# A first gather with the one-hot rows held still, products of no use in the routing's waits, and p loaded in another step

## The chip, the cores and the metric

The kernel runs on one core of one Trainium2 chip. Its time is what the device takes for one launch, in microseconds; of several runs the median is given. TensorE (PE in the rows, with its weight loads as PEld), VectorE (DVE), ScalarE (ACT), GpSimd (POOL) and SyncE (SP) run their own instructions in their own order and wait for each other by semaphores. SP issues nearly all transfers, on one queue.

## The reference, cut to what matters

One layer over 512 tokens of 1024 channels, in float32:

```
merged = sigmoid(gate_pool) * (A @ w_pu) + sigmoid(gate_attn) * (B @ w_au)
x   = LayerNorm(alpha * x + merged @ w_o)
moe = for each token: top 1 of 4 groups, then top 2 of its 8 experts;
      h = silu(x @ w_eg[e]) * (x @ w_eu[e]);  y += (h @ w_ed[e]) * weight
ple = sigmoid(x @ w_pg) * (p @ w_pp)
x   = LayerNorm(alpha * x + moe + ple)
```

There are 32 experts, each with 6 MB of weights (`w_eg` and `w_eu` are 1024 x 512, `w_ed` is 512 x 1024). All of them are read whatever the tokens choose. p has 512 x 256 numbers, `w_pg` 1024 x 1024.

## The kernel before, in words

Tokens stand in four blocks of 128. Most operands outside the experts are kept as two parts, high and low (type fp32r in the rows), whose products are added. Up to 343 us the kernel makes the projections, both mixers and the output projection, whose last blocks are interleaved with the first norm and the routing.

**Routing** (lines 910 to 1001, in an order written out by hand). `normalise` scales a block; `turn` transposes it; `route` multiplies it by the router's weights; `keep_high` (ACT) and `keep_low` (an engine named by the caller) store its high and low parts in `x1`, in the order that the experts' weights want. `choose` finds group and experts for two blocks at a time on DVE and ends with `msk`, the 0/1 choice; `place` counts a token's place in its expert by products with a triangle of ones; `one_hots` makes `G`, 0/1 rows that say which token goes to which slot. `count_tokens` and `rank` order the experts by tokens, `weigh` makes the weights, `relabel` turns both into the order by rank.

**Gather.** A unit has 128 slots, for two, three or four experts. `gather` multiplies: x1's 128 channels are the stationary operand and `G`, 128 slots wide, is moved, so the result has channels in partitions, as the experts' products need it. For unit 0 that is 8 channel blocks x 4 token blocks x 2 parts = 64 products. Four PSUM banks are opened by a product with zeros each (`open_bank`), half of the sum is made before blocks 2 and 3 are chosen (around `choose` and `place`), the rest behind `one_hots` of these blocks. `keep_slots` scales and shifts the result into `xg`. The first expert product (`inner(0, 0)`) follows in pieces.

**Experts** (`pair`). There are twelve units: `inner` makes h's two factors with the slots stationary and the weights moving, 8 k-steps each; four transposes turn h; `outer` makes the output, whose pieces are added to `acc` by `scatter_steps` in the next unit. In even units the next two units' slots are gathered between the outer products: two banks behind f = 1, two behind f = 3. In units 0 and 1 `renew` builds `acc` anew from `x1`.

**Weights.** Each expert comes in six chunks of 1 MB. A chunk's load is issued by SP when `eload_past` is told that TensorE has used up an older chunk, into that one's buffer. Loads stand on SP in the order in which the code calls for them. Sixteen buffers serve, of which eight are of the kind `s8`; the dictionary `KEEP` says from which step (unit, place in the unit) on how many of these eight are withheld from the chunks.

**Embedding** (`embedding`, a generator). `EMB` says how many of its steps run at each of six places of a unit: 0 between the halves of the first product, 1 behind it, 2 between the halves of the second, 3 behind h's transposes, 4 behind f = 1, 5 at the end. Step 1 loads p (`pr`) and begins to add x1's parts on POOL; step 2 transposes p and loads the first quarter of `w_pg` and `w_pp`; steps 3 to 6 transpose x1; step 7 makes high and low parts of the quarter (`split`: a copy on ACT, a subtraction on POOL) and loads the next one; then four steps of products, and so on for four quarters.

Of the kernel before, what the change touches and what calls it, by code (L numbers as in the profile page):

```python
# [37 lines left out]
def layer_kernel(ctx: ExitStack, tc: tile.TileContext, x, p, w_in, w_pool, pool_scale, w_pu, w_au,  # L38
# [18 lines left out]
    def mm(name="mm"):  # L57
        return ps.tile([128, 512], F32, name=name, tag="mm", bufs=4)
# [625 lines left out]

    def rank(ct, at, rcol):

        o = zz("rk_ps")
        nc.tensor.matmul(o[:, :E], ecol[:E].to_broadcast([E, 128]), at[:E], start=True, stop=True)
        nc.tensor.matmul(o[:, E:2 * E], rcol[:E].to_broadcast([E, 128]), ident[:E, :E], start=True, stop=True)
        nc.vector.tensor_copy(order, o[:, :E])  # L690
        rk, over = (lnt.tile([128, E], F32, name=n, tag=t) for n, t in (("rk", "fold"), ("over", "i8")))
        nc.vector.tensor_copy(rk, o[:, E:2 * E])

        nc.vector.tensor_scalar(room, rk, BIG - 0.5, float(CAP // 2), op0=OP.is_lt, op1=OP.mult)
        nc.vector.tensor_scalar(over, rk, E - FIXED - 0.5, float(CAP // 2), op0=OP.is_gt, op1=OP.mult)
        nc.vector.scalar_tensor_tensor(room, room, float(CAP // 2), over, op0=OP.add, op1=OP.add)
        nc.vector.tensor_sub(over, ct[:, :E], room)
        countf = lnt.tile([128, 1], F32, name="countf")
        nc.vector.tensor_reduce(countf, over, axis=AX.X, op=OP.max)
        nc.vector.tensor_scalar(countf, countf, 0.0, None, op0=OP.max)  # L700
        nc.vector.tensor_copy(count, countf)
        return rk

# [128 lines left out]

    def gather(G, o, kb, tbs):

        whole = len(tbs) == NT
        n = G[0].shape[2] * 128
        for kx in range(2):
            cs = slice((2 * kb + kx) * 128, (2 * kb + kx + 1) * 128)
            for tb in tbs:
                for i in range(2):  # L840
                    nc.tensor.matmul(o[:, kx * 256:kx * 256 + n], x1[tb][:, i, cs],  # L841
                                     G[tb // 2][:, tb % 2].rearrange("p u s -> p (u s)"),
                                     start=whole and tb == i == 0,
                                     stop=tb == NT - 1 and i == 1 and (whole or kx == 1))

    def open_bank(o):

        nc.tensor.matmul(o, strict[:, :1].to_broadcast([128, 128]), strict[:, None].to_broadcast([128, 4, 128]),
                         start=True, stop=False)

# [59 lines left out]
    with tc.manual_schedule():  # L910
# [47 lines left out]
        normalise(3)  # L958
        xs = [mm("xg_ps") for _ in range(4)]
        for o in xs:  # L960
            open_bank(o)
        route(2)
        keep_high(1, (1,))
        keep_low(1, 0, pool)
        keep_low(1, 1, dve)
        one_hots(G[0], (0,), 0)
        turn(3)
        keep_high(2)
        keep_low(2, 0, pool)
        route(3)  # L970
        xtp_cm.__exit__(None, None, None)
# [4 lines left out]
        fold_logits(lg2, 3)  # L976
        for kb in range(2):
            gather(G, xs[kb], kb, (0, 1))
        keep_high(3)
        keep_low(2, 1, dve)  # L980
        choose(lg2, 2)
        keep_low(3, 0, pool)
        place(2)
        keep_low(3, 1, dve)
        eload_first(17)
        for kb in range(2, 4):
            gather(G, xs[kb], kb, (0, 1))
        G.append(lnt.tile([128, 2, 1, 128], F32R, name="G", tag="wr2"))
        one_hots(G[1], (0,), 2)
        counted = count_tokens()  # L990
        slots_of((0,))
        for kb in range(4):
            gather(G, xs[kb], kb, (2, 3))
            keep_slots((0,), xs[kb], kb)
            if kb == 1:
                first = mm()
                rk = rank(*counted)
            if kb:
                inner(0, 0, first, range(2 * kb - 2, 2 * kb))
        inner(0, 0, first, range(6, 8))  # L1000
        relabel(rk, weigh())
# [6 lines left out]
    def pair(j, other, extra):  # L1008
# [76 lines left out]
        for f in range(4):  # L1085
            for c in range(2):
                outer(j, hT, f, c, o[c])
            if f % 2:
                eload_past(chunk0[j] + n_experts[j] * (4 + (f + 1) // 2))
            if m and f % 2:  # L1090
                og = [zz("xg_ps") for _ in range(2)]
                for i in range(2):
                    gather(G, og[i], f - 1 + i, range(NT))
                    keep_slots(m, og[i], f - 1 + i)
            if f == 1:
                embed(4)
                Gt, ws = turn_one_hots(Gw)
        embed(5)
        y = [weighted(o[c], ws) for c in range(2)]
# [47 lines left out]
    def embedding():  # L1147
# [58 lines left out]
        def split(raw):  # L1206
            hi = s8([128, KD, 256], F32R, "pgh"), ex.tile([128, 2, 256], F32R, name="pph", bufs=1)
            lo = s8([128, KD, 256], F32R, "pgl"), ex.tile([128, 2, 256], F32R, name="ppl", bufs=1)
            for r, h, l in zip(raw, hi, lo):
                nc.scalar.activation(h, r, AF.Copy)  # L1210
                nc.gpsimd.tensor_sub(l, r, h.bitcast(F32))  # L1211
            return hi, lo
# [56 lines left out]

    EMB = {3: (0, 0, 0, 1, 0, 0), 4: (1, 1, 1, 1, 1, 1), 5: (2, 2, 1, 2, 2, 1), 6: (2, 2, 1, 2, 1, 1)}  # L1270

    KEEP = {(2, 5): 2, (3, 1): 4, (3, 5): 5, (4, 0): 6, (4, 1): 7, (4, 2): 8}
    with tc.manual_schedule():
# [124 lines left out]
```

## Time and profile before

| | us |
|---|---|
| median of three runs | 877.06 (876.9 to 878.21) |
| profiled execution, its own time | 878.82 |
| its span in the trace | 877.1 |
| mean granted TensorE clock | 0.956 |

PE is busy 812.8 us of the span, DVE 429.1, ACT 228.4, POOL 174.5. The queue of SP carries 241.11 MB. A granted clock of 1.00 is 2.4 GHz, 0.50 is 1.2 GHz. In the rows a matmul in plain float32 (the experts' products) stands as two records; those of the high and low parts as one. A matmul's time in a row runs to the end of its pipeline, so neighbours overlap, and a group of them takes less than the sum. A number in brackets at the end of a row is the engine's idle time before it, and behind the arrow who ended it. The chain that ended last shows for a transfer when it was issued and how long it took to land, its time in the queue with it.

### The profile page before, as it was taken

To read this page: it belongs to the slowest core of one execution; us is meant where nothing else is said; L and a number is where in the kernel's file an instruction comes from. 1 tells how busy PE (TensorE), PEld (TensorE's weight loads), DVE (VectorE), ACT (ScalarE), POOL (GpSimd) and SP (SyncE) were. 2 spreads that over 40 slices of the span, in tenths; PEclk is the share of its full clock that TensorE was granted. 3 is DMA by queue.
4 is the path that set the end of the run, shared out by engine and by line. 5 is a ranking of instruction groups with operands and counts; after the bars stand their busy time and mean duration, and the time that the engine had idled before them with its cause. 6 is when DMAs were issued, how large, how long until landed. Compare 5 with 4: busy or idle time off the path is not lost.

```text
span 877.1 us, 11632 instructions
## 1 busy us (share of the span) xinstructions
PE 812.8 (93%) x4454; PEld 515.6 (59%) x4454; DVE 429.1 (49%) x746; ACT 228.4 (26%) x471; POOL 174.5 (20%) x165
## 2 busy tenths in 40 slices
PE   8999899899999999998999778799899999999983
PEld 7886677677768887734354334476375744545422
DVE  5278647545458756457742446322113243443337
ACT  3123444444461115213202011220211201210314
POOL 3333324224221222100002020212313000000135
PEclk9999999999999999599999988899899999999997
DMA  7431131212114695576999999999999999999992
GB/s 252 142 97 49 48 96 49 82 63 87 58 49 167 178 382 206 228 287 247 421 420 419 417 406 419 371 405 375 418 411 399 407 419 418 420 420 419 412 370 99
DMA packets 66076, 241.91 MB, mean 276 GB/s; under 512 B 12384, under 2 KB 32864, under 8 KB 41696
## 3 DMA queue, kind: packets, MB, share of 16 engines
q1 hardware_dynamic: 66016, 241.11, 70.7%
q8 instruction: 37, 0.61, 0.3%
q14 instruction: 23, 0.19, 0.1%
HBM read 239.00 MB, written 2.10 MB: 275 GB/s over the span
## 4 chain that ended last, share of the span: by engine, by line
PE 29%; DMA 18%; DVE 2%; issue 2%; POOL 1%; ACT 1%; SPq 1%; POOLq 0%; DVEq 0%; ACTq 0%
PE mm L905 11%; DMA ew<-in_w_eu_dram 8%; PE mm L1110 7%; DMA ew<-in_w_eg_dram 4%; PE xg_ps L841 4%; DMA ew<-in_w_ed_dram 3%; PE sc_ps L1143 3%; DMA pr<-in_p_dram 2%; PE pg_ps L143 1%; PE pg_ps L144 1%; PE pg_ps L145 1%; POOL pgl L1211 1%; SPq L538 0%; PE hT_ps L1057 0%; PE gt_ps L882 0%
## 5 line engine op out<-in xcount | busy, mean ns | idle before, releaser
L905 PE MATMUL mm<-ew,xg 128*32 128x512 f32 (+1 forms) x1088 | 189.6, 632 | 12.2 <-DMA ew<-in_w_eu_dram 8.6
L905 PEld LDWEIGHTS mm<-ew,xg 128*32 128x32 f32 (+1 forms) x1088 | 54.5, 126 | 132.4 <-issue 107.7
L1110 PE MATMUL mm<-ew,hT 128*32 128x512 f32 (+1 forms) x544 | 93.2, 611 | 2.1 <-DMA ew<-in_w_ed_dram 1.1
L143 PE MATMUL mm<-xth,whi 128*128 128x512 f32 x224 | 91.6, 409 | 0.0
L132 POOL TENSOR_TENSOR wlo<-wraw,whi 128x1024 fp32r<-128x1024 f32 x23 | 69.0, 3000 | 106.3 <-DVE whi L127 52.2
L145 PE MATMUL mm<-xth,wlo 128*128 128x512 f32 x224 | 88.7, 396 | 0.0
L144 PE MATMUL mm<-xtl,whi 128*128 128x512 f32 x224 | 88.3, 394 | 0.0
L1042 DVE TENSOR_TENSOR h<-mm,h 128x512 f32<-128x512 f32 x24 | 16.6, 692 | 106.8 <-PE mm L905 55.5
L841 PEld LDWEIGHTS xg_ps<-G,x 128*128 128x128 f32 x448 | 59.6, 207 | 15.5 <-issue 12.3
L841 PE MATMUL xg_ps<-G,x 128*128 128x256 f32 (+1 forms) x448 | 62.6, 300 | 2.4 <-DVE xg L861 2.4
L1144 DVE TENSOR_TENSOR acc<-acc,sc_ps 128x512 f32<-128x512 f32 x88 | 54.7, 682 | 6.6 <-PE sc_ps L1143 6.0
L1110 PEld LDWEIGHTS mm<-ew,hT 128*32 128x32 f32 (+1 forms) x544 | 25.1, 122 | 54.7 <-issue 47.5
L143 PEld LDWEIGHTS mm<-xth,whi 128*128 128x128 f32 x224 | 42.8, 191 | 9.5 <-issue 0.9
L144 PEld LDWEIGHTS mm<-xtl,whi 128*128 128x128 f32 x224 | 43.0, 192 | 8.8 <-issue 0.5
L145 PEld LDWEIGHTS mm<-xth,wlo 128*128 128x128 f32 x224 | 42.6, 190 | 9.4
L859 ACT ACTIVATE xg<-xg_ps,bq,gq 128x128 f32<-128x128 f32 x56 | 24.7, 456 | 89.2 <-PE xg_ps L841 79.5
L127 DVE CAST whi<-wraw 128x2048 fp32r<-128x2048 f32 x22 | 26.9, 1225 | 33.8 <-PE mm L144 16.6
L132 DVE TENSOR_TENSOR wlo<-wraw,whi 128x1024 fp32r<-128x1024 f32 x23 | 40.7, 1769 | 1.0
L144 PE MATMUL pg_ps<-pgl,xT 128*128 128x256 f32 x128 | 37.0, 289 | 4.0 <-POOL pgl L1211 4.0
L1159 POOL TENSOR_TENSOR xf<-x 128x1024 f32<-128x1024 f32 x4 | 9.4, 2371 | 149.4 <-PE mm L905 120.9
L1231 DVE TENSOR_TENSOR sg<-pg_ps,sg 128x256 f32<-128x256 f32 x16 | 6.8, 425 | 66.0 <-ACT sg L1230 66.0
L1143 PE MATMUL sc_ps<-yh,Gt 128*128 128x512 f32 x88 | 37.8, 430 | 1.1 <-DVE sg L1231 1.1
(269 smaller groups left out, 1357.8 us busy)
## 6 DMA issues: line engine op xcount, KB each, us to landing
ew<-in_w_eg_dram SPq DMA_DIRECT2D x64, 1024.0 KB, 15.3
ew<-in_w_eu_dram SPq DMA_DIRECT2D x64, 1024.0 KB, 14.0
ew<-in_w_ed_dram SPq DMA_DIRECT2D x62, 1024.0 KB, 14.0
wraw<-in_w_in_dram SPq DMA_DIRECT2D x15, 1024.0 KB, 5.6
wraw<-in_w_o_dram SPq DMA_DIRECT2D x4, 1024.0 KB, 5.0
pgr<-in_w_pg_dram SPq DMA_DIRECT2D x4, 1024.0 KB, 16.4
wraw<-in_w_pu_dram SPq DMA_DIRECT2D x2, 1024.0 KB, 4.9
wraw<-in_w_au_dram SPq DMA_DIRECT2D x2, 1024.0 KB, 5.0
```

The costliest lines, as they stand in the source:

```text
L127: nc.vector.tensor_copy(hi, wraw[i])
L132: eng.tensor_sub(lo[:, j], wraw[i][:, j], hi[:, j].bitcast(F32))
L143: nc.tensor.matmul(o, lh, rh, start=start, stop=False)
L144: nc.tensor.matmul(o, lh, rl, start=False, stop=False)
L145: nc.tensor.matmul(o, ll, rh, start=False, stop=stop)
L841: nc.tensor.matmul(o[:, kx * 256:kx * 256 + n], x1[tb][:, i, cs], G[tb // 2][:, tb % 2].rearrange("p u s -> p (u s)"), start=whole and tb ...
L859: nc.scalar.activation(xgs[us[0]][:, k], o[:, i, 0], AF.Identity, scale=gq[:, k:k + 1], bias=bq[:, k:k + 1])
L905: nc.tensor.matmul(o[cs], xgs[j][:, k, cs], ew[chunk0[j] + ne * (2 * n + k // 4) + i][:, k % 4], start=k == 0, stop=k == KD - 1)
L1042: nc.vector.tensor_mul(ht, o, ht)
L1110: nc.tensor.matmul(o[cs], hT[:, f, cs], ew[chunk0[j] + ne * (4 + f // 2) + i][:, f % 2, halves[c]], start=f == 0, stop=f == 3)
L1143: nc.tensor.matmul(o, Gt[:, tb * 128:(tb + 1) * 128], y[c][i], start=i == 0, stop=i == 1)
L1144: nc.vector.tensor_add(acc[tb][:, cs], acc[tb][:, cs], o)
```

## The change

The first gather is turned round: `gather_rows` holds the one-hot rows of a token block still (128 tokens x 128 slots) and moves 512 channels of `x1`, so the result has slots in partitions, in two banks. `turn_rows` then transposes it, in two halves of four transposes, and scales and shifts it into `xg`, alternately on ACT and DVE. The first expert product follows in one piece.

`busy(n)` runs n products of 512 columns into a bank that nobody reads: four before `route(2)`, four before `turn(3)`, five before `route(3)`, ten before `place(2)`, three before the second half of the gather. Two `keep_low` calls move from DVE to POOL, so that POOL has four in a row. `rank` is split: the capacity check (`measure`) runs behind the first expert product in the code.

In unit 0 the gathers for units 1 and 2 come behind all outer products, with one bank at a time. In `split`, half of the `w_pg` subtraction goes to DVE. p's step moves from unit 3, place 3, to unit 3, place 0; the first `split` from unit 4, place 5, to place 4; `KEEP` withholds buffers earlier.

```diff
-    def rank(ct, at, rcol):
+    def rank(at, rcol):
...
+        rk = lnt.tile([128, E], F32, name="rk", tag="fold")
         nc.vector.tensor_copy(rk, o[:, E:2 * E])
+        return rk
+
+    def measure(ct, rk):
...
-    def open_bank(o):
-        nc.tensor.matmul(o, strict[:, :1].to_broadcast([128, 128]), strict[:, None].to_broadcast([128, 4, 128]),
-                         start=True, stop=False)
+    def gather_rows(G, o, c, tbs):
+        for tb in tbs:
+            for i in range(2):
+                nc.tensor.matmul(o[c], G[tb // 2][:, tb % 2, 0], x1[tb][:, i, halves[c]], start=tb == i == 0,
+                                 stop=tb == NT - 1 and i == 1)
+
+    def turn_rows(rows, h):
+        pt = tt("xgT_ps")
+        for k in range(4):
+            nc.tensor.transpose(pt[:, k * 128:(k + 1) * 128], rows[:, (4 * h + k) * 128:(4 * h + k + 1) * 128], ident)
+        for i in range(4):
+            k = 4 * h + i
+            src, g, b = pt[:, i * 128:(i + 1) * 128], gq[:, k:k + 1], bq[:, k:k + 1]
+            if i % 2:
+                nc.vector.tensor_scalar(xgs[0][:, k], src, g, b, op0=OP.mult, op1=OP.add)
+            else:
+                nc.scalar.activation(xgs[0][:, k], src, AF.Identity, scale=g, bias=b)
+
+    def busy(n):
+        for _ in range(n):
+            nc.tensor.matmul(spare, strict, strict[:, None].to_broadcast([128, 4, 128]), start=True, stop=True)
...
-        xs = [mm("xg_ps") for _ in range(4)]
-        for o in xs:
-            open_bank(o)
+        spare = mm("spare_ps")
+        xs = [mm("xg_ps") for _ in range(2)]
+        busy(4)
         route(2)
...
         one_hots(G[0], (0,), 0)
+        busy(4)
         turn(3)
         keep_high(2)
         keep_low(2, 0, pool)
+        busy(5)
         route(3)
...
-        for kb in range(2):
-            gather(G, xs[kb], kb, (0, 1))
         keep_high(3)
-        keep_low(2, 1, dve)
+        keep_low(2, 1, pool)
+        for c in range(2):
+            gather_rows(G, xs, c, (0, 1))
         choose(lg2, 2)
         keep_low(3, 0, pool)
+        keep_low(3, 1, pool)
+        busy(10)
         place(2)
-        keep_low(3, 1, dve)
         eload_first(17)
-        for kb in range(2, 4):
-            gather(G, xs[kb], kb, (0, 1))
...
-        for kb in range(4):
-            gather(G, xs[kb], kb, (2, 3))
-            keep_slots((0,), xs[kb], kb)
-            if kb == 1:
-                first = mm()
-                rk = rank(*counted)
-            if kb:
-                inner(0, 0, first, range(2 * kb - 2, 2 * kb))
-        inner(0, 0, first, range(6, 8))
+        rows = lnt.tile([128, D], F32, name="rows")
+        busy(3)
+        for c in range(2):
+            gather_rows(G, xs, c, (2, 3))
+            if c:
+                nc.vector.tensor_copy(rows[:, halves[c]], xs[c])
+            else:
+                nc.scalar.activation(rows[:, halves[c]], xs[c], AF.Copy)
+        turn_rows(rows, 0)
+        rk = rank(*counted[1:])
+        turn_rows(rows, 1)
+        first = mm()
+        inner(0, 0, first, range(KD))
+        measure(counted[0], rk)
         relabel(rk, weigh())
...
-            if m and f % 2:
+            if m and j and f % 2:
...
+        if j == 0:
+            for kb in range(4):
+                og = zz("xg_ps")
+                gather(G, og, kb)
+                keep_slots(m, og, kb)
         embed(5)
...
-            for r, h, l in zip(raw, hi, lo):
+            parts = [(t[0][:, :4], t[0][:, 4:], t[1]) for t in (raw, hi, lo)]
+            for r, h, l, eng in zip(*parts, (nc.gpsimd, nc.vector, nc.gpsimd)):
                 nc.scalar.activation(h, r, AF.Copy)
-                nc.gpsimd.tensor_sub(l, r, h.bitcast(F32))
+                eng.tensor_sub(l, r, h.bitcast(F32))
...
-    EMB = {3: (0, 0, 0, 1, 0, 0), 4: (1, 1, 1, 1, 1, 1), 5: (2, 2, 1, 2, 2, 1), 6: (2, 2, 1, 2, 1, 1)}
-    KEEP = {(2, 5): 2, (3, 1): 4, (3, 5): 5, (4, 0): 6, (4, 1): 7, (4, 2): 8}
+    EMB = {3: (1, 0, 0, 0, 0, 0), 4: (1, 1, 1, 1, 2, 0), 5: (2, 2, 1, 2, 2, 1), 6: (2, 2, 1, 2, 1, 1)}
+    KEEP = {(2, 2): 2, (3, 1): 4, (3, 3): 5, (3, 5): 6, (4, 0): 7, (4, 1): 8}
```

## Rows read from the trace of the kernel before

**Rows 1.** Stages; busy us of each engine, then granted clock, DMA share, GB/s
```profile
353.00:366.00 13.00, 12.25 (x57) 12.09 (x58) 7.16 (x31) 2.63 (x4) 1.54 (x1) 0.50 0.82 318
366.00:376.60 10.60, 10.60 (x32) 4.61 (x31) 1.59 (x11) 1.61 (x4) 0.00 (x0) 0.50 0.01 5
...
412.00:541.00 129.00, 115.22 (x702) 49.94 (x691) 64.58 (x110) 18.45 (x31) 9.39 (x4) 0.93 1.01 411
541.00:700.00 159.00, 145.46 (x1086) 96.21 (x1082) 42.97 (x85) 29.45 (x51) 34.19 (x23) 0.96 0.99 398
700.00:850.00 150.00, 146.65 (x797) 67.28 (x798) 60.24 (x99) 24.19 (x46) 10.36 (x9) 0.99 1.01 417
```

**Rows 2.** Timeline of SP's issues: start us, us, engine, line
```profile
376.62 1.25 SPq L538 DMA_DIRECT2D ew<-in_w_eg_dram  x2
...
567.23 0.58 SPq L1153 DMA_DIRECT2D pgr<-in_w_pg_dram  x1
```

**Rows 3.** Timeline of PE, routing and unit 0; idle before in brackets
```profile
344.58 1.16 PE L848 MATMUL xg_ps<-strict 128*128 128x512 f32 x4
...
347.55 1.37 PE L594 MATMUL x1T_ps<-ident,acc 128*128 128x128 f32 x8 [0.47 <-ACT acc L769]
...
353.31 3.65 PE L841 MATMUL xg_ps<-G,x 128*128 128x128 f32 x16
...
367.41 3.68 PE L905 MATMUL mm<-ew,xg 128*64 128x512 f32 x8
...
377.57 10.52 PE L905 MATMUL mm<-ew,xg 128*64 128x512 f32 x48
...
404.40 4.07 PE L841 MATMUL xg_ps<-G,x 128*128 128x256 f32 x32 [2.42 <-DVE xg L861]
```

**Rows 4.** Timeline of PE in unit 4
```profile
507.55 1.94 PE L1188 MATMUL pT_ps<-ident,pr 128*128 128x128 f32 x8 [8.73 <-DMA pr<-in_p_dram]
...
528.55 1.94 PE L905 MATMUL mm<-ew,xg 128*32 128x512 f32 x8 [4.38 <-DMA ew<-in_w_eu_dram]
```

**Rows 5.** The page's costliest groups: busy us, mean ns, then idle before
```profile
L1042 DVE TENSOR_TENSOR h<-mm,h 128x512 f32<-128x512 f32 x24 | 16.6, 692 | 106.8 <-PE mm L905 55.5
...
L859 ACT ACTIVATE xg<-xg_ps,bq,gq 128x128 f32<-128x128 f32 x56 | 24.7, 456 | 89.2 <-PE xg_ps L841 79.5
...
L144 PE MATMUL pg_ps<-pgl,xT 128*128 128x256 f32 x128 | 37.0, 289 | 4.0 <-POOL pgl L1211 4.0
```

**Rows 6.** Timeline of DVE, routing of blocks 2 and 3, relabelling
```profile
349.36 1.06 DVE L782 TENSOR_TENSOR x<-acc,x 128x512 fp32r<-128x512 f32 x1 [2.71 <-ACT x L779]
...
352.15 1.74 DVE L782 TENSOR_TENSOR x<-acc,x 128x512 fp32r<-128x512 f32 x1 [0.20 <-ACT x L779]
...
354.61 0.96 DVE L641 CAST gif<-gi 128x2 f32<-128x2 uint32 x1
...
357.35 0.22 DVE L655 TENSOR_TENSOR msk<-oh 128x64 fp32r<-128x64 f32 x1
...
378.73 0.25 DVE L712 RECIPROCAL rc<-sgm 128x16 f32<-128x16 f32 x1 [9.42 <-ACT sgm L711]
...
383.86 0.29 DVE L740 TENSOR_TENSOR ranked<-by_slot 128x128 f32<-128x128 f32 x1
```

**Rows 7.** Timeline of POOL
```profile
351.30 1.55 POOL L782 TENSOR_TENSOR x<-acc,x 128x512 fp32r<-128x512 f32 x1 [3.09 <-ACT x L779]
354.01 1.54 POOL L782 TENSOR_TENSOR x<-acc,x 128x512 fp32r<-128x512 f32 x1 [1.16 <-ACT x L779]
...
562.70 4.51 POOL L1211 TENSOR_TENSOR pgl<-pgr,pgh 128x2048 fp32r<-128x2048 f32 x1 [48.37 <-DMA ew<-in_w_eg_dram]
```

**Rows 8.** Chain that ended last: start us, us, what
```profile
468.62 19.84 DMA ew<-in_w_eg_dram
488.48 18.94 DMA pr<-in_p_dram
...
510.06 18.44 DMA ew<-in_w_eu_dram
```

More of the change, by code (lines that the diff above doesn't have):

```diff
@@ L690, in rank @@
         nc.vector.tensor_copy(order, o[:, :E])
-        rk, over = (lnt.tile([128, E], F32, name=n, tag=t) for n, t in (("rk", "fold"), ("over", "i8")))
+        rk = lnt.tile([128, E], F32, name="rk", tag="fold")
         nc.vector.tensor_copy(rk, o[:, E:2 * E])
+        return rk
+    def measure(ct, rk):
+        over = lnt.tile([128, E], F32, name="over", tag="i8")
         nc.vector.tensor_scalar(room, rk, BIG - 0.5, float(CAP // 2), op0=OP.is_lt, op1=OP.mult)
@@ L701, in rank @@
         nc.vector.tensor_copy(count, countf)
-        return rk
     def weigh():
@@ L831, in one_hots, with gather @@
                                         pos[:, b:b + 2, :, None].to_broadcast(shape), op=OP.is_equal)
-    def gather(G, o, kb, tbs):
-        whole = len(tbs) == NT
+    def gather(G, o, kb):
         n = G[0].shape[2] * 128
@@ L838, in gather @@
             cs = slice((2 * kb + kx) * 128, (2 * kb + kx + 1) * 128)
-            for tb in tbs:
+            for tb in range(NT):
                 for i in range(2):
@@ L842, in gather @@
                                      G[tb // 2][:, tb % 2].rearrange("p u s -> p (u s)"),
-                                     start=whole and tb == i == 0,
-                                     stop=tb == NT - 1 and i == 1 and (whole or kx == 1))
-    def open_bank(o):
-        nc.tensor.matmul(o, strict[:, :1].to_broadcast([128, 128]), strict[:, None].to_broadcast([128, 4, 128]),
-                         start=True, stop=False)
+                                     start=tb == i == 0, stop=tb == NT - 1 and i == 1)
+    def gather_rows(G, o, c, tbs):
[17 more added lines that the diff above has]
+            nc.tensor.matmul(spare, strict, strict[:, None].to_broadcast([128, 4, 128]), start=True, stop=True)
     def slots_of(us):
@@ L1089, in pair @@
                 eload_past(chunk0[j] + n_experts[j] * (4 + (f + 1) // 2))
-            if m and f % 2:
+            if m and j and f % 2:
                 og = [zz("xg_ps") for _ in range(2)]
                 for i in range(2):
-                    gather(G, og[i], f - 1 + i, range(NT))
+                    gather(G, og[i], f - 1 + i)
                     keep_slots(m, og[i], f - 1 + i)
```

## The prediction

> **What bounds the kernel now.** I read the table by stages first. From 412 us to 850 us the DMA share stays near 1.0 at 398 to 417 GB/s [rows 1]: the experts' weights arrive at the rate the queue can give, and the end follows the last of them. So microseconds count where the queue runs dry, and the same table shows where: from 366.0 to 376.6 its share is 0.01 [rows 1]. Every weight buffer is full then, and the next load is issued at 376.62, when unit 0's first four k-steps have ended on TensorE [rows 2]. What holds TensorE back is the second thing to see in the table: its granted clock is 0.50 (the lower level, 1.2 GHz) from 353 to 376.6 [rows 1], while it is busy almost without a break. Before that it had short idle stretches behind the last transposes (one of 0.47 us in [rows 3]) and narrow products. Third come the waits later on: 8.73 us until p has landed, 4.38 us for an expert chunk [rows 4], 4.0 us for POOL's subtraction of the embedding weights [rows 5]. Because the queue is full there, they cost time only as far as they empty it.
>
> The profiled execution took 878.82 us (span 877.1, so 1.7 us lie around it), 1.76 us over the median of 877.06. I work out a difference against the span and take it from the median.
>
> **First gather, up to the first expert product.** It now takes 16 products of 512 columns in place of 64 of 128 columns. Before, 16 narrow ones took 3.65 us at the lower clock [rows 3], so 64 cost 14.6 us, half of them behind the second half of the routing. A wide one at full clock: four took 1.16 us [rows 3], less the tail that overlaps, about 0.25 us each. So 2.1 us for eight, and eight of the sixteen lie beside the choice of experts, as the old ones did.
>
> Now the path, counted from the release of `msk`. The choice of experts ends at 357.35 + 0.22 = 357.57 [rows 6]; the first half of unit 0's first product ends when the load at 376.62 is issued [rows 2]: 19.05 us. Afterwards, at full clock:
> - place, positions, one-hots: 1.5 us. They took 357.57 to about 360.3, with one `keep_low` in between (1.06 us a piece [rows 6]) that moves to POOL, and with their products at half clock.
> - counting and the three products of no use: 0.6 us more on TensorE. (The four at first take the place of four that opened banks, 1.16 us [rows 3]; four and five more fill waits for ACT and DVE.)
> - eight wide products 2.1 us; the second half's copy out of PSUM 0.7 (a 128x512 one takes 692 ns on DVE [rows 5]); four transposes 0.6 (eight took 1.37 with a wait in them [rows 3]).
> - four k-steps, 16 records: 48 took 10.52 us [rows 3], so 3.5 us.
>
> Sum 9.0 us, a saving of 10.0. The other four k-steps took 3.5 us at full clock already, but in the old order 1.0 us of gather stood between (376.6 to 377.57 [rows 2, 3]): the first product is ready 11.0 us sooner. The scaling copies from the transposes are new. ACT and DVE share a bank and will probably alternate, 8 x 0.46 us [rows 5] = 3.7 us, but TensorE needs 0.88 us per k-step (four records), so it stays the slower of the two and hides them. Without that cover they would cost 3.2 us, all but the first.
>
> `choose` starts about 0.4 us sooner, since the 1.74 us subtraction in front of it leaves DVE [rows 6]. The ten products of no use (2.5 us) end at about 357.3 and lie beside `choose`; so they cost nothing at full clock. But four subtractions now run on POOL back to back, and that has a price. The DVE subtraction at 352.15 took 1.74 us against 1.06 at 349.36, and ended 1.06 us after POOL's own one ended at 352.85; the cast at 354.61 took 0.96 us and ended with POOL's at 355.55 [rows 6, 7]. So DVE's two-input operations and casts wait for POOL's. `choose` has seven such, POOL three subtractions left: from nothing to 2 x 1.55 = 3.1 us more. I take 0.2, near the lower end, since POOL's subtractions are few and most of `choose` is one-input work; so 11.0 + 0.4 - 0.2 = 11.2 us, with the ends 8.3 and 12 (the 0.6 us of counting hidden).
>
> The Trainium skill (GPSIMD Engine Reference, section Specifications) says that POOL shares its SBUF interfaces with VectorE, in contention with instructions of two SBUF inputs or in a two-port mode. The trace agrees (1.74 against 1.06 us); by the rule each of the seven could wait, so its sum is 8.3.
>
> **What follows in unit 0.** DVE's rank, capacity and relabelling work goes behind the copies: about 1.3 + 0.5 us, then 378.73 to 384.15, 5.4 us [rows 6]. It ends near 372.5, before unit 0's second product (about 376.7), so it stays hidden; it has 3 us of slack before SiLU is late. Gathering for units 1 and 2 behind all of unit 0's outer products: TensorE waited 2.42 us there for DVE's scaling [rows 3], which is queued behind the renewal of x1. DVE sets this end before and after, so it is worth 0 for TensorE; two chunks are loaded some 4 us sooner, but the queue runs dry behind them again until unit 1's first product. So 11.2 us arrive at 412 unchanged.
>
> **p and the embedding.** p's load moves from j = 3, step 3 to step 0. It was issued at 488.48 and landed 18.94 us later, behind a queue 20 us deep [rows 8]. In unit 3's first half it stands behind the fourth of unit 4's first eight loads; the second was issued at 468.62 [rows 8] and they go out every 2.5 us, so p goes at about 476 (in old time) and lands near 496, ahead of the transposes (507.55 - 8.73 = 498.8 [rows 4]): the 8.73 us wait goes. POOL's additions that move with it find POOL idle. What is late next is the expert chunks: p passes five of them, which land its 1.25 us later, so that those for the next half are there at 468.62 + 19.84 + 6 x 2.5 + 1.25 = 504.7, the next four at 515, and the last of the second product at 510.06 + 18.44 = 528.5, where TensorE waited 4.38 us anyway [rows 4, 8]. The queue was full throughout (1.01 [rows 1]). So this is worth 0; ends -1 (two buffers less from j = 2 on) and +2.
>
> `split` gives half of the 4.51 us subtraction [rows 7] to DVE, and its first one moves ahead of unit 4's last outer products. That takes away the 4.0 us wait [rows 5] and lets SP pass: SP issued the next embedding load at 567.23 only, when POOL was done [rows 2], with loads behind it. In return four expert loads now stand behind that issue and come about 2 us later. In 541 to 700 the queue moved 398 GB/s against 417 later [rows 1]: 159 x (1 - 398/417) = 7.2 us lost in all. I follow it through unit 5: embedding load and four chunks are in at about 574 in both orders, the next group comes 1.9 us sooner, and the one after 2.5. I take 2.3; ends -1 and 6.
>
> **Sum:** 11.2 + 0 + 2.3 = 13.5 us, 877.06 - 13.5 = 863.6. From 700 on TensorE has hardly a wait and the queue is full [rows 1]; both start sooner by the same amount, and the tail is unchanged.
>
> **Rivals.**
> - The clock falls all the same, for a while, between 352 and 360. For it: route's products stay narrow. Against it: 13 wide products fill the stretches, and wide expert products, begun at 367.41, were what TensorE ran when the clock came back [rows 1, 3]. Up to 5 us of work stretches to twice its length: 3 us less, 866.6. Chance 0.14. The Trainium skill (TensorE: Matmul & The Clock Gate, Part 1) lays the clock to how busy the engine is. The trace bears out half: from 353.31 to 367.41 TensorE was busy with narrow products nearly without a break, and the clock stayed at 0.50 [rows 1, 3].
> - POOL holds DVE at every operation: 2.9 us less (3.1 for 0.2), 866.5. Chance 0.12.
> - p and the embedding free the queue fully: 16 to 17 us in all, 860.5. For it: 7.2 us are lost there. Against it: the loads of pg. Chance 0.09.
> - Slower: the clock stays at half through the whole path and the products of no use become its longest part. Eight wide and ten useless ones from 353.3 on take 18 x 0.43 = 7.7 us, so TensorE reaches `place` at 361.0, not 357.3; place, positions and one-hots until 363.0, counting and three more until 365.2, eight wide until 368.9, copy and transposes until 370.5. Eight k-steps at half clock (8 records took 3.68 us [rows 3], 32 take 14.7) end at 385.2 against 381.1 before: +4.1 us, 881.2. It decides from a granted clock of 0.50 that still stands at 378. Against it: wide expert products were running when the clock came back. Chance 0.04.
> - It doesn't do what it says (a buffer conflict stalls the gather, worth about 11 us): 877. Chance 0.03.
>
> **Chances.** The forecast has 0.58, at 861 to 866. Faster by over 0.2% (1.75 us, what can be told from no change) 0.93, within it 0.03, slower 0.04. The range 859 to 869 takes in the rivals but the last two, and most of a clock that falls for longer.
>
> **What would show it.** Right: granted clock 1.00 through 353 to 377; next load issued near 366; dry time before it 1 to 3 us, not 11; the gathers for units 1 and 2 ended near 397 (404.40 + 4.07 = 408.5 before [rows 3]); no wait for p, but waits for chunks near 493 and 504 instead; no 4 us wait for `pgl`. Wrong: a clock of 0.50 after 353, casts of over a microsecond in `choose`, a DMA share under 0.95 between 412 and 530, or the time from 700 to the end changed.

## The result and the profile after

The changed kernel takes 868.02 us (median), the kernel before beside it 877.63. Three executions in this document were disturbed and count in no ratio: one of the four of the changed kernel here (1118 us; the others lie from 867.4 to 868.04), one of the kernel before in the first group of experiments (3615 us), and one of the experiment on unit 0's gather (1300 us). The ratio of the two kernels is 0.9886, with 0.9867 to 0.9905 as the 95% interval. So the change is faster, by 9.6 us between the medians, and the forecast of 863.6 was 4.4 us too low: inside the range of 859 to 869, above the 861 to 866 that had a chance of 0.58. The profiled execution took 868.04 us (span 866.3, 10.8 less than the span before).

The stages of the changed kernel, in the columns of [rows 1]:

```profile
353.00:366.00 13.00, 11.34 (x59) 8.34 (x61) 9.35 (x35) 3.98 (x7) 4.45 (x3) 1.00 0.80 315
366.00:376.60 10.60, 10.60 (x52) 3.56 (x50) 7.31 (x28) 1.16 (x4) 0.00 (x0) 1.00 0.72 273
...
412.00:541.00 129.00, 114.75 (x660) 51.53 (x656) 62.93 (x120) 20.14 (x35) 9.35 (x4) 0.98 1.02 417
541.00:700.00 159.00, 148.49 (x1090) 93.50 (x1084) 49.83 (x79) 28.48 (x52) 30.05 (x24) 0.99 0.99 403
```

The granted clock is 1.00 where it was 0.50, and the stretch in which the queue was dry, 366 to 376.6, now has a DMA share of 0.72 instead of 0.01. SP's issues of the changed kernel show the new place of the first late load and of the embedding's load:

```profile
368.10 3.77 SPq L538 DMA_DIRECT2D ew<-in_w_eg_dram  x3
...
547.89 0.59 SPq L1185 DMA_DIRECT2D pgr<-in_w_pg_dram  x1
549.66 2.58 SPq L538 DMA_DIRECT2D ew<-in_w_eg_dram  x4
```

The first was 376.62 before [rows 2], so 8.5 us are won there, and by 412 the chunks land 9.6 us earlier, steadily up to 548. TensorE's timeline through routing and unit 0 (line 852 the wide gather, 870 the products of no use, 926 the expert product):

```profile
353.17 2.10 PE L852 MATMUL xg_ps<-x,G 128*128 128x512 f32 x8
355.11 2.45 PE L870 MATMUL spare_ps<-strict 128*128 128x512 f32 x10
359.22 0.27 PE L661 MATMUL pos_ps<-msk,strict 128*128 128x64 f32 x1 [1.66 <-DVE msk L655]
...
360.88 2.02 PE L852 MATMUL xg_ps<-x,G 128*128 128x512 f32 x8
...
364.42 13.95 PE L926 MATMUL mm<-ew,xg 128*64 128x512 f32 x64
...
394.73 4.06 PE L844 MATMUL xg_ps<-G,x 128*128 128x256 f32 x32 [2.32 <-DVE xg L882]
```

The durations are as forecast, but the wait in the third row is not: the ten products end at 357.6 and TensorE still waits 1.66 us for `msk`. VectorE's timeline in `choose`, and POOL's beside it, say why:

```profile
353.38 0.24 DVE L636 TENSOR_TENSOR lg<-lg_ps,lbias 128x80 f32<-128x80 f32 x1 [1.37 <-PE lg_ps L619]
353.66 0.24 DVE L638 MAX8 gm<-lg 128x8 f32<-128x8 f32 x2
...
354.08 0.16 DVE L640 FIND_INDEX8 gi<-gm,lg 128x8 uint32<-128x8 f32 x1
354.27 0.17 DVE L641 CAST gif<-gi 128x2 f32<-128x2 uint32 x1
354.48 1.47 DVE L642 TENSOR_TENSOR pen<-iota_e,gif 128x8 f32<-128x8 f32 x1
355.98 1.55 DVE L644 SCALAR_TENSOR_TENSOR sel<-pen,lg 128x64 f32<-128x64 f32 x1
...
358.85 0.22 DVE L655 TENSOR_TENSOR msk<-oh 128x64 fp32r<-128x64 f32 x1
```
```profile
351.32 6.13 POOL L786 TENSOR_TENSOR x<-acc,x 128x512 fp32r<-128x512 f32 x4 [3.09 <-ACT x L783]
```

POOL's four subtractions run from 351.32 to 357.45, 1.53 us each, so one ends at 355.92 and the last at 357.45. The two VectorE instructions of 1.47 and 1.55 us end at 355.95 and 357.53, each with one of POOL's. From logits to `msk` it takes 5.69 us (353.38 to 359.07), where before it took 3.86 (353.72 to 357.58, `msk`'s row in [rows 6]), from this row on:

```profile
353.72 0.24 DVE L636 TENSOR_TENSOR lg<-lg_ps,lbias 128x80 f32<-128x80 f32 x1
```

In unit 4 TensorE's wait for p is gone and waits for chunks stand where it was, as forecast:

```profile
495.37 3.62 PE L926 MATMUL mm<-ew,xg 128*32 128x512 f32 x26 [1.45 <-DMA ew<-in_w_eg_dram]
...
505.35 3.62 PE L926 MATMUL mm<-ew,xg 128*32 128x512 f32 x26 [1.46 <-DMA ew<-in_w_eu_dram]
...
516.42 1.82 PE L926 MATMUL mm<-ew,xg 128*32 128x512 f32 x2 [4.53 <-DMA ew<-in_w_eu_dram]
```

### The profile page after: what moved, and what is told of

Same layout as the page of the kernel before. It is cut to its first block, busy times and chain, and to the rows that moved or that the text cites. A ratio compares the mean times of both kernels' runs of the same rounds, so it can differ in the third digit from the quotient of the medians.

```text
span 866.3 us, 11612 instructions
## 1 busy us (share of the span) xinstructions
PE 804.1 (93%) x4436; PEld 506.0 (58%) x4436; DVE 441.4 (51%) x753; ACT 227.6 (26%) x472; POOL 172.8 (20%) x167
## 4 chain that ended last, share of the span: by engine, by line
PE 35%; DMA 14%; DVE 2%; issue 2%; SPq 1%; POOL 0%; ACT 0%; POOLq 0%; DVEq 0%; ACTq 0%
PE mm L926 13%; PE mm L1142 9%; DMA ew<-in_w_eu_dram 7%; PE xg_ps L844 5%; PE sc_ps L1175 3%; DMA ew<-in_w_eg_dram 3%; DMA ew<-in_w_ed_dram 3%; PE pg_ps L143 1%; PE pg_ps L145 1%; PE pg_ps L144 1%; PE gt_ps L903 1%; SPq L538 1%; PE hT_ps L1084 0%; DVE acc L915 0%; DVE outs L1293 0%
## 5 line engine op out<-in xcount | busy, mean ns | idle before, releaser
L844 PEld LDWEIGHTS xg_ps<-G,x 128*128 128x128 f32 x384 | 46.2, 189 | 11.5 <-issue 7.4
L844 PE MATMUL xg_ps<-G,x 128*128 128x256 f32 (+1 forms) x384 | 48.5, 283 | 2.3 <-DVE xg L882 2.3
L880 ACT ACTIVATE xg<-xg_ps,bq,gq 128x128 f32<-128x128 f32 x48 | 21.3, 456 | 68.4 <-PE xg_ps L844 58.1
L1164 POOL TENSOR_TENSOR accl<-acc,acch 128x512 fp32r<-128x512 f32 x8 | 10.5, 1343 | 136.3 <-ACT acch L1163 136.3
L143 PE MATMUL pg_ps<-pgh,xT 128*128 128x256 f32 x128 | 37.0, 289 | 0.2
L243 ACT ACTIVATE sp<-sp 128x128 f32<-128x128 f32 (+3 forms) x32 | 14.4, 468 | 86.7 <-POOL sp L241 86.7
```

Of the source, the lines that this page charges most:

```text
L143: nc.tensor.matmul(o, lh, rh, start=start, stop=False)
L880: nc.scalar.activation(xgs[us[0]][:, k], o[:, i, 0], AF.Identity, scale=gq[:, k:k + 1], bias=bq[:, k:k + 1])
```

## Experiments

Each was timed beside the kernel before on the same chip, in three groups; a ratio is to that kernel there (about 878.4 us in each group).

**No products of no use.**
```diff
-        busy(4)
...
-        busy(4)
...
-        busy(5)
...
-        busy(10)
...
-        busy(3)
```


> All products of no use are taken out; everything else is as changed. Theory (these products hold TensorE's clock): the granted clock falls to 0.50 near 352.6 us again, the wide products, transposes and the first expert product run at half clock until expert products have been running for some us; the load behind unit 0's first four k-steps is issued at 371 to 374 us, not at 368.1, and the time is 3 to 6 us longer than the changed kernel's 868.0. Rival (the wide gather itself keeps or brings back the clock, and the extra products are worth nothing): clock 1.00 or one short fall, load issued by 368.6, time within 0.5 us of the changed kernel's.

871.73 us, ratio 0.9917 (0.9896 to 0.9938). The windows of this run, columns as in [rows 1], then TensorE's second half of the gather and first expert product, then SP's first late load:

```profile
350.00:353.00 3.00, 1.97 (x19) 1.39 (x19) 2.06 (x4) 2.58 (x5) 1.59 (x2) 0.94 1.03 415
353.00:366.00 13.00, 10.78 (x32) 8.27 (x32) 8.01 (x30) 2.58 (x4) 4.43 (x3) 0.50 0.81 315
366.00:368.00 2.00, 2.00 (x12) 1.29 (x14) 1.12 (x5) 1.24 (x3) 0.00 (x0) 0.92 0.00 0
366.00:376.60 10.60, 10.60 (x52) 4.16 (x54) 7.96 (x32) 2.12 (x7) 0.00 (x0) 0.98 0.42 145
```
```profile
361.19 3.78 PE L852 MATMUL xg_ps<-x,G 128*128 128x512 f32 x8
...
367.15 13.95 PE L921 MATMUL mm<-ew,xg 128*64 128x512 f32 x64
```
```profile
370.83 2.04 SPq L538 DMA_DIRECT2D ew<-in_w_eg_dram  x2
```

The clock is at half before the wide gather begins, as before, and the load is 2.7 us later than with the products. But from `msk` to the load it takes 11.6 us (359.25 to 370.83), where the kernel before took 19.05. The clock is back soon after 366 (0.92 from 366 to 368), ahead of the first expert product at 367.15: the wide half of the gather and the transposes were what TensorE had run. In the kernel before it stayed at 0.50 until 376.6, with narrow products among the first expert products [rows 1]. The products of no use are worth some 3 us, 871.73 against 868.0 to 868.6; the rest of the gain does without them.

**Those products alone, in the kernel before, with its narrow gather.** The half of the gather that stood behind `place` moves ahead of it.
```diff
-        for o in xs:
-            open_bank(o)
+        busy(xs[3], 4)
...
+        busy(xs[3], 4)
...
+        busy(xs[3], 5)
+        for o in xs:
+            open_bank(o)
...
-        for kb in range(2):
+        for kb in range(4):
             gather(G, xs[kb], kb, (0, 1))
...
+        busy(tt("spare_ps"), 5)
...
+        busy(tt("spare_ps"), 3)
```


> The kernel before with its narrow gather (64 products of 128 columns), and the products of no use put into the same waits (4, 4, 5, then 5 beside choose since the narrow products take longer there, then 3). Embedding, p and keep_low as before. Theory (what unit 0 gained is the clock, not the turned gather): clock 1.00 from 353 to 377, the narrow products take about 0.11 us each, the next load is issued near 367 and the first expert product ends near 370; the time is 9 to 10 us under the kernel before, about 868, of which nothing comes from the embedding. Rival (the turned gather is the gain): with narrow products the clock falls in spite of the extra ones, or they stay slow; load issued at 372 or later, gain under 6 us.

873.32 us, ratio 0.9931 (0.991 to 0.9952), with its four runs from 870.38 to 879.32; the profiled one is the longest. Windows and TensorE's timeline of that run:

```profile
350.00:353.00 3.00, 2.67 (x27) 2.39 (x25) 2.73 (x9) 2.59 (x4) 1.85 (x2) 1.00 0.98 363
353.00:356.00 3.00, 3.00 (x19) 3.00 (x18) 2.74 (x13) 0.22 (x1) 0.93 (x1) 0.59 0.87 289
```
```profile
351.50 5.24 PE L841 MATMUL xg_ps<-G,x 128*128 128x128 f32 x32
```

With the fillers the clock stands at 1.00 until 353, and then it falls in the middle of 32 narrow products, with TensorE busy for 3.00 of 3.00 us. In this execution the late load goes out at 373.17, and counted from where the stretch starts (1.7 us earlier than in the trace of the kernel before) the chunks arrive as late as there: the second theory, for this execution. What gave the other three 5 to 8 us stays open; this trace does not show it. Their mean granted clocks over the whole kernel are 0.976, 0.976 and 0.966, against 0.966 here, so in two of them the clock may have held in this stretch too. By its median the run lies between the theories.

**The early fillers only.**
```diff
-        busy(10)
...
-        busy(3)
```


> The changed kernel without its two late groups of filling products (ten in the wait for msk, three behind place), the three early groups kept; what is computed is the same. Without any filling products the clock fell at 352.8 and the late load came 11.6 us after msk instead of 9.0. Theory: the wait for msk by itself is enough to lower the clock, so it falls between 355 and 359, the load comes 10.5 to 11.6 us after msk and the end is 2 to 4 us later than the changed kernel's. Rival: the early groups are what counts, the clock stays at 1.00 to 366, the load comes 9.0 us after msk, and the end is within 0.5 us.

871.73 us, ratio 0.9921 (0.9904 to 0.9938), 3.1 us over the changed kernel beside it:

```profile
356.00:359.00 3.00, 0.00 (x0) 0.00 (x0) 2.86 (x11) 0.00 (x0) 1.68 (x2) 1.00 0.91 341
359.00:362.00 3.00, 2.55 (x11) 2.37 (x12) 1.73 (x9) 0.00 (x0) 0.00 (x0) 0.63 0.99 415
362.00:366.00 4.00, 4.00 (x14) 2.99 (x12) 1.21 (x4) 1.00 (x2) 0.00 (x0) 0.50 0.53 221
```
```profile
372.43 1.25 SPq L538 DMA_DIRECT2D ew<-in_w_eg_dram  x2
```

TensorE waits 3.9 us for `msk` with nothing to do, and behind that idle stretch the clock is at half. The load comes 13.1 us after `msk` (359.30), later than either theory had it; the time is the first theory's. It costs as much as no fillers at all.

**p's load at its old step.**
```diff
-    EMB = {3: (1, 0, 0, 0, 0, 0), 4: (1, 1, 1, 1, 2, 0), 5: (2, 2, 1, 2, 2, 1), 6: (2, 2, 1, 2, 1, 1)}
+    EMB = {3: (0, 0, 0, 1, 0, 0), 4: (1, 1, 1, 1, 2, 0), 5: (2, 2, 1, 2, 2, 1), 6: (2, 2, 1, 2, 1, 1)}
```


> The changed kernel with p's step back in unit 3, place 3; KEEP and the first split's place as changed. Theory (the wait for p is hidden, since the transfer queue is full there): TensorE waits some 7 to 9 us for p again, then less for chunks; expert chunks from the end of unit 4 on land within 0.3 us of the changed kernel's; time within 0.5 us of its 868.0. Rival (p's early load gave the 1.5 us that the chunks gained between 541 and 700 us): the time is 1 us or more longer.

869.13 us, ratio 0.9898 (0.9881 to 0.9916), against 0.9886 and, in a second group, 0.9889 (0.9871 to 0.9906; 868.64 us) for the changed kernel. TensorE's row in unit 4 here:

```profile
495.99 1.94 PE L1220 MATMUL pT_ps<-ident,pr 128*128 128x128 f32 x8 [8.50 <-DMA pr<-in_p_dram]
```

The wait of 8.5 us is back, the 1.45 us waits of before 510 are gone, the DMA share from 412 to 541 is 1.02 in both, and from 530 on the chunks stand to the changed kernel's as they did before the wait. p's step is worth 0 in the trace; the ratios differ by about 1 us, which they cannot tell from nothing (866.44 to 870.2 here).

**The changed kernel again.** Unaltered, in the second group.

> The changed kernel itself, unaltered, beside the next three on one chip, so that differences of a microsecond can be told. Its ratio to the kernel before was 0.9886 (0.9867 to 0.9905). Theory: the same again, 868 us, the first late load issued 9.0 us after msk is done, clock 1.00 from 353 to 376. Rival (the gain was partly that execution): 870 or more.

868.64 us, ratio 0.9889. The first theory; its first late load comes 9.0 us after `msk` too (358.34 and 367.37).

**Unit 0's gather between its outer products.**
```diff
-            if m and j and f % 2:
+            if m and f % 2:
```


> The changed kernel with unit 0's inner order as before: groups of 8 narrow gather products (128 columns) for units 1 and 2 stand between unit 0's groups of 8 wide ones, instead of 32 and 32 in a block behind unit 0's last product. Theory: eight narrow products at full clock are 1.1 us (the eight of 376.53 took that), so the first late load is 10.1 us after msk instead of 9.0, the clock stays at 1.00 from 366 to 376.6, and the end is within 1.0 us of the changed kernel. Rival: narrow products pull the clock down even between wide ones, as the trace without wide gathers showed for 32 of them in a row; the granted clock is 0.5 in part of 366 to 376.6, the load is 11.5 us or more after msk, and the end is 2 to 4 us later.

868.4 us (median of four, 867.19 to 870.6), ratio 0.9899 (0.9879 to 0.9919): no difference that can be told. My expectation put the narrow products into unit 0's first product; this line moves them into its second one, behind the load. So the load (367.49) could not move, and it tells of the second product alone:

```profile
383.53 4.10 PE L844 MATMUL xg_ps<-G,x 128*128 128x256 f32 x32
...
394.07 4.07 PE L844 MATMUL xg_ps<-G,x 128*128 128x256 f32 x32 [2.42 <-DVE xg L882]
```

In either order TensorE waits 2.3 to 2.4 us for VectorE's scaling, and the last gather ends at 398.1 here and 398.8 in the changed kernel; the forecast's 0 for it holds.

**POOL's subtractions moved to VectorE's waits.**
```diff
-        keep_low(2, 0, pool)
+        keep_low(2, 0, dve)
...
-        keep_low(3, 0, pool)
-        keep_low(3, 1, pool)
-        busy(10)
-        place(2)
+        busy(7)
+        place(2, lambda: keep_low(3, 0, dve))
...
         one_hots(G[1], (0,), 2)
+        keep_low(3, 1, dve)
```
The late gather also goes block by block, and the load behind `place` is issued after the moved subtractions.

> The changed kernel, but three of POOL's four subtractions in a row go to DVE, into its waits: keep_low(2, 0) ahead of choose, keep_low(3, 0) behind place's products, keep_low(3, 1) behind the one-hots; POOL keeps keep_low(2, 1). Seven products of no use instead of ten; the second half of the gather takes block 2 for both halves first. Theory (POOL's subtractions held DVE inside choose for 1.47 - 0.17 and 1.55 - 0.23 us): the operations at L642 and L644 take about 0.2 us each, msk is ready near 356.6 and not 359.07, the load behind unit 0's first four k-steps is issued 2 to 2.5 us sooner, near 365.8, and the time is about 866. Rival (something else sets the end of choose or of the gather): choose ends no sooner, or the gain is taken by the subtractions on DVE; time within 0.5 us of 868.

866.73 us, ratio 0.9862 (0.9845 to 0.988). The two held instructions take 0.17 and 0.23 us, from logits to `msk` it is 3.08 us (355.02 to 358.10), and from logits to the late load (367.59) 12.6 us, where the changed kernel took 14.7 (353.38 to 368.10). This execution reached the logits 1.6 us later, so the load does not stand near 365.8 as the theory had it, but it is as much sooner on its path. By the ratios the gain is some 2 us, with intervals that overlap.

**Only the last two moved, behind `place`'s first step.**
```diff
-        keep_low(3, 0, pool)
-        keep_low(3, 1, pool)
         busy(10)
         place(2)
+        keep_low(3, 0, dve)
+        keep_low(3, 1, dve)
```


> The changed kernel with the last two of POOL's four subtractions of the routing (the low halves of token block 3) done by VectorE after the positions' first step, so that POOL has two left and is done some 3 us earlier. Theory: VectorE is held by POOL's running subtraction wherever it has two inputs in SBUF, so without the last two the two held instructions of 1.47 and 1.55 us shrink, msk is done 1.5 us or more sooner after the logits than 5.7 us; but VectorE then does 2.1 us more between msk and the first load, so the load comes within 1 us of the changed kernel's and the time within 1 us of 868. Rival (the two instructions are long for another reason): msk 5.7 us after the logits as before, and the time 1 to 2 us above 868.

867.24 us, ratio 0.9869 (0.985 to 0.9889). It is not told apart from the changed kernel. `choose` takes 3.06 us (352.05 to 355.11), but TensorE's ten products run until 356 and VectorE then spends 1.99 us on the two subtractions: the load comes at 366.47, 14.4 us after the logits. As the theory had it: what holds VectorE is POOL's running subtraction, and taking it away pays only if the work finds a wait to hide in.

**Both tables of the embedding as before.**
```diff
-    EMB = {3: (1, 0, 0, 0, 0, 0), 4: (1, 1, 1, 1, 2, 0), 5: (2, 2, 1, 2, 2, 1), 6: (2, 2, 1, 2, 1, 1)}
+    EMB = {3: (0, 0, 0, 1, 0, 0), 4: (1, 1, 1, 1, 1, 1), 5: (2, 2, 1, 2, 2, 1), 6: (2, 2, 1, 2, 1, 1)}
-    KEEP = {(2, 2): 2, (3, 1): 4, (3, 3): 5, (3, 5): 6, (4, 0): 7, (4, 1): 8}
+    KEEP = {(2, 5): 2, (3, 1): 4, (3, 5): 5, (4, 0): 6, (4, 1): 7, (4, 2): 8}
```


> The changed kernel with the split of the embedding's work over the steps as it was before (both tables old), all else changed. In the two traces the weight chunks landed 9.6 us earlier up to 548 and 11.1 us earlier from 600 on, so I put the split's worth at 1.5 us, where the prediction had 2.3. Theory: 1.0 to 2.0 us longer than the changed kernel run beside it; chunks land level with it to about 545 and 1.2 to 1.9 us later from 600 on, and the 4 us wait of TensorE for pgl is back. Prediction's term: 2.3 longer. Rival (the 1.5 was what differs from one execution to the next): within 0.5 us, no step in the landings.

866.06 us, ratio 0.9867 (0.9851 to 0.9884): 2.6 us faster than the changed kernel, where all the theories had it slower or level. They all fell. From 548 to the end its chunks gain 3.8 us on the kernel before, those of the changed kernel 1.5: the stage's small gain is the sum of a gain and a loss. The next two runs take them apart.

**One entry of the table as before.**
```diff
-    EMB = {3: (1, 0, 0, 0, 0, 0), 4: (1, 1, 1, 1, 2, 0), 5: (2, 2, 1, 2, 2, 1), 6: (2, 2, 1, 2, 1, 1)}
+    EMB = {3: (1, 0, 0, 0, 0, 0), 4: (1, 1, 1, 1, 1, 1), 5: (2, 2, 1, 2, 2, 1), 6: (2, 2, 1, 2, 1, 1)}
```


> The changed kernel with one entry of one table as before: in unit 4 the split of pgr, and with it the issue of the next pgr, is back at step 5 from step 4. p's early load and the new points at which buffers are kept stay. Theory: the cost of 2.6 us that the old tables took away comes from this entry alone: at step 4 the issue of pgr waits on SP for pgl and holds back the four chunk loads that stand behind it, and the DMA share from 541 to 550 was 0.77 instead of 1.00. So the share there is 1.00 again and the ratio is 0.986 to 0.9875, like that with both tables old. Rival: the kept buffers do it (fewer chunks ahead), and it stays at 0.9885 to 0.989 with a share under 0.85.

865.49 us, ratio 0.9856 (0.9839 to 0.9872). First the window of the changed kernel and VectorE's half of `pgl` there, then window and SP's issues of this one:

```profile
541.00:550.00 9.00, 9.00 (x68) 5.17 (x64) 6.41 (x11) 4.13 (x7) 4.61 (x2) 0.84 0.73 295
```
```profile
545.26 2.56 DVE L1244 TENSOR_TENSOR pgl<-pgr,pgh 128x1024 fp32r<-128x1024 f32 x1 [1.26 <-ACT pgh L1243]
```
```profile
541.00:550.00 9.00, 9.00 (x70) 5.06 (x64) 4.10 (x10) 2.01 (x4) 0.00 (x0) 0.86 1.00 399
```
```profile
545.31 2.12 SPq L538 DMA_DIRECT2D ew<-in_w_eg_dram  x4
555.35 0.59 SPq L1185 DMA_DIRECT2D pgr<-in_w_pg_dram  x1
```

With the entry as before, SP issues four chunk loads at 545.31, and the embedding's load afterwards. In the changed kernel the embedding's load stands first in SP's queue and waits there until 547.89, when VectorE's half of `pgl` (545.26 to 547.82) has read the last quarter out of its buffer, and the same four chunks go out at 549.66; in between the queue runs dry. From 548 to the end the chunks gain 4.4 us here, 1.5 in the changed kernel. That one entry costs 2.6 to 3 us, and the buffers that are kept earlier, which stay in this run, are not the cause.

**The halves of `pgl` alone, in the kernel before.**
```diff
-            for r, h, l in zip(raw, hi, lo):
+            parts = [(t[0][:, :4], t[0][:, 4:], t[1]) for t in (raw, hi, lo)]
+            for r, h, l, eng in zip(*parts, (nc.gpsimd, nc.vector, nc.gpsimd)):
-                nc.gpsimd.tensor_sub(l, r, h.bitcast(F32))
+                eng.tensor_sub(l, r, h.bitcast(F32))
```


> The kernel before with one part of the change alone: pgl's subtraction cut into a half on POOL and a half on VectorE. Theory: it is this part that gains in the embedding's stage. TensorE's wait of 4.0 us for pgl falls to about 1, the issue of the next pgr, which waited for pgl until 567.2, comes some 2 us earlier, the DMA share between 556 and 576 rises from 0.93 to 1.0, and the time is 2.5 to 3.7 us below the kernel before (ratio 0.9958 to 0.9972). Rival: with the old late start of unit 0 the stage has slack, and it is worth under 1 us.

873.22 us, ratio 0.9937 (0.9925 to 0.995), some 5 us, more than any theory gave it. TensorE's wait and SP's issue in this run, then its first late load and a window of its routing, which is that of the kernel before:

```profile
562.31 0.39 PE L144 MATMUL pg_ps<-pgl,xT 128*128 128x256 f32 x1 [1.04 <-POOL pgl L1212]
```
```profile
563.40 0.58 SPq L1153 DMA_DIRECT2D pgr<-in_w_pg_dram  x1
```
```profile
373.04 8.39 SPq L538 DMA_DIRECT2D ew<-in_w_eg_dram  x4
```
```profile
366.00:376.60 10.60, 10.60 (x46) 4.47 (x47) 2.87 (x18) 1.98 (x7) 0.00 (x0) 0.80 0.23 78
```

The wait is 1.04 us instead of 4.0 [rows 5], and the chunks, 1.9 us ahead of the kernel before at 548, are 5.9 ahead at the end: 4.0 us come from here; of the 1.9, 1.4 are there at 342, ahead of all that was changed. The old routing is not equally slow in every execution: here the clock is back sooner (0.80 from 366 to 376.6, against 0.50 in [rows 1]), and from `msk` to the late load it takes 16.65 us (356.40 to 373.04), not 19.05. By 412 the chunks have kept 0.5 us of that.

**Both repairs together.** Three subtractions of the routing on VectorE, both tables as before, the halves kept.

> The changed kernel with both repairs that the runs so far suggest: three of POOL's four subtractions of the routing moved to VectorE, into its waits (that alone: ratio 0.9862 to the kernel before), and both of the embedding's tables as before (that alone: 0.9867), the halves of pgl kept between POOL and VectorE. Theory: they lie in different stretches and add up, the first worth 1 to 2 us of the start of unit 0 and the second 2.6 us near 550, so 863.5 to 865.5 us, ratio 0.983 to 0.985. Rival: the queue of chunk loads takes back what the earlier start gives, so no better than 0.9867 within 0.0005.

864.11 us (863.25 to 865.15), ratio 0.9837 (0.9824 to 0.9851): the fastest, and 4 us below the changed kernel. Two rows of VectorE's `choose` and SP's first late load here:

```profile
353.91 0.17 DVE L642 TENSOR_TENSOR pen<-iota_e,gif 128x8 f32<-128x8 f32 x1
354.12 0.23 DVE L644 SCALAR_TENSOR_TENSOR sel<-pen,lg 128x64 f32<-128x64 f32 x1
```
```profile
365.37 3.77 SPq L538 DMA_DIRECT2D ew<-in_w_eg_dram  x3
```

The two add up, as the theory had it.

## Why the prediction was right in direction and short in size

- **The path was right, and the clock is a part of it.** With the wide gather, the first product in one piece and the clock at 1.00, the path from `msk` to the late load takes 9.03 us (359.07 to 368.10), forecast 9.0. Gather, counting, transposes, copies: no term of that sum was off by more than some tenths. It took 19.05 before, and 11.6 without the products of no use, at 0.50 until soon after 366: 7.5 of the 10.0 us come without them, 2.6 with them. How the 7.5 divide between fewer records and a clock that is back sooner, no run shows; part of it belongs to the traced execution of before, as another with the old routing took 16.65.
- **What holds the clock.** The late fillers are needed: without them it fell behind the wait for `msk`. All nine traced executions with the wide gather and fillers in all the waits kept 1.00 from 353 to 376. That a narrow gather cannot keep it rests on one execution, the slowest of four. The argument that "wide expert products were running when the clock came back" was no more than what one trace had: without fillers it was back ahead of the first of them.
- **The step that failed: POOL's price in `choose`.** I wrote "from nothing to 2 x 1.55 = 3.1 us more. I take 0.2, near the lower end, since POOL's subtractions are few and most of `choose` is one-input work". `choose` grew by 1.83 us. So unit 0's start gave 9.6 us and not 11.2. With POOL's last two subtractions moved `choose` takes 3.06 us, so POOL's share of it was 0.8 us before and 2.6 after. The rival "POOL holds DVE at every operation" priced it at 3.1, and the truth lay between: POOL had 4.1 us of work left when `choose` began, and two instructions were caught, each until one of POOL's subtractions ended. The row that should have decided was in hand: the cast that ended with POOL's subtraction [rows 6, 7]. The number of POOL's subtractions still to end, each with one instruction caught, was the size. The Trainium skill (GPSIMD Engine Reference, section Specifications) names this contention for instructions with two SBUF inputs or in a two-port mode. The trace agrees on the two that were held, while `MAX8` and `FIND_INDEX8` ran at 0.16 to 0.24 us beside POOL; the cast of before, held too (0.96 us), has one input, and no row shows its mode. The sum by that rule, 8.3 us with all seven held, was too low. (VectorE's subtraction of [rows 6] ended 1.04 us after POOL's, not 1.06; nothing rests on it.)
- **The embedding, 2.3 forecast, 1.2 in the trace** (9.6 of the 10.8 us of span lie ahead of 541). Its two parts were of opposite sign. The halves are worth about 4; the earlier step costs 2.6 to 3, since "four expert loads now stand behind that issue and come about 2 us later" was followed for the chunks of unit 5 but not for the queue, which runs dry meanwhile (0.73 from 541 to 550). That the net came within 1.1 us of the measured one is in part luck, since the gain of the halves was put too small and the dry stretch was left out.
- **p at 0** held, with the waits for chunks at the places named.
- **The rest of the 4.4 us** is not in the difference of the two traces: I took a difference of spans from the median of 877.06, while the profiled execution of before was 1.76 us over it. 1.6, 1.1 and 1.76 make 4.46. The mean granted clock of that execution, 0.956, is as low as any of the kernel before's (0.956 to 0.962).
- "Casts of over a microsecond in `choose`" was the right kind of sign, on the wrong instruction: the cast took 0.17 us, as it ended with a subtraction of POOL's by chance of its start.

## What to carry to other kernels

Where POOL's instructions can hold VectorE's, count how many of POOL's are still to end when a chain of small ones begins on VectorE: here each of the last two held one of the chain to its own end. Moved into VectorE's waits they shortened the chain by 2.6 us (5.69 to 3.08); moved onto VectorE's path they won as much and cost nearly all of it again (14.4 us from logits to load, against 14.7). A change that slips fillers into waits to hold a clock is tested with some of them left out: leaving out the late ones cost as much as leaving out all. A load that waits for a buffer must not be put ahead of loads that could go: look at the one queue they share, not only at when each is wanted. When a stage with two edits shows a small gain, run each alone; here about +4 and -2.6 to -3 were hidden in 1.2.

## What the runs showed of the hardware that I had not expected

- TensorE's granted clock fell from 1.00 to 0.50 while the engine was busy for 3.00 of 3.00 us with products of 128 columns (353 to 356, fillers with the old gather, one execution), and stayed at 1.00 through wide ones in nine. The Trainium skill (TensorE: Matmul & The Clock Gate, Part 1) lays the clock to how busy the engine is; by busy time alone, this trace differs.
- The same 32 gather products behind a wait of 2.3 us took 4.06 us in one execution of the changed kernel and, in another, more:

```profile
394.02 5.56 PE L844 MATMUL xg_ps<-G,x 128*128 128x256 f32 x32 [2.34 <-DVE xg L882]
```

  The granted clock of 376.6 to 412 was 1.00 in the first and 0.95 in the second; the two executions (868.04 and 868.64 us) hardly differ.
- POOL is held by VectorE too: in the last experiment its subtraction, begun beside one of VectorE's, took 2.21 us instead of 1.53.

```profile
351.36 1.05 DVE L788 TENSOR_TENSOR x<-acc,x 128x512 fp32r<-128x512 f32 x1
```
```profile
351.64 2.21 POOL L788 TENSOR_TENSOR x<-acc,x 128x512 fp32r<-128x512 f32 x1 [3.98 <-ACT x L785]
```
